# Two layers of a hybrid transformer on one core: row traffic on other queues, modulation weights in half pieces

## The chip, the cores and the metric

The kernel runs on one core of a Trainium2 chip. The metric is the device time of one execution in microseconds (us), taken as the median of the runs. The core has five engines that each work through their own instructions in order and wait for each other by semaphores: TensorE (PE) multiplies matrices into PSUM, VectorE (DVE) and ScalarE (ACT) do element work, GpSimd (POOL) does element work in SBUF, and SyncE (SP) only issues transfers (DMAs). ACT and POOL can issue transfers too. A transfer that has to wait holds up whatever stands behind it on the engine that issues it.

## The reference, cut to what matters

There are 512 latent tokens and 128 context tokens of width 1024, and two layers. In each layer every token gets a modulated normalisation, `rms_norm(x, g) * (1 + scale) + shift`, then one input projection, then four token mixers side by side, then an output projection and a SwiGLU block.

- **Modulation.** `silu(cond) @ w_mod + b_mod` gives six vectors of 1024 per group (shift, scale and gate for both halves of a layer). `w_mod` is 1024 by 6144 per layer, so it is a big weight for two rows of input.
- **Gated DeltaNet.** Keys, queries and values go through a short convolution. Per chunk of 64 tokens a triangular system has to be inverted, and then a scan runs over the chunks. This is a long chain of small steps.
- **Latent attention (MLA).** The input projection gives 256 columns of compressed query, 128 of compressed keys and values and 32 of a rotary key. The first two are RMS-normalised: a row of a token is multiplied by one number for the 256 columns and one for the 128 columns. The 32 columns of the latent tokens are rotated.
- Grouped attention and neighbourhood attention (NA) read further columns of the projection.

All of it is float32.

## The kernel before, in words

Features lie on the partitions and tokens in the free dimension (640 tokens, 512 latent and 128 context). Big products are made as three float32r products of split operands: a weight tile is loaded into `wst`, ACT writes its high part `whi` (line 308) and DVE its low part `wlo` (line 309).

**What sets the order.** The order of TensorE's instructions is written out when the program is built. In the mixer a planner (`_Order`) runs generators as tasks. Each task has a rank (a low one goes first), each step of PE advances a clock, `yield t` lets a task wait for a time of that clock, `yield "w", 1` lets it wait for a PSUM bank, and `od.via(("DMA", 2.8))` books an engine for so long and returns when it is done. PE then works through this order strictly; where an operand is late, PE stands still. The order on the other engines and queues is made by the framework's own scheduler around PE's order. Rank 0 is the DeltaNet chain (`delta_chain`), 0.4 the modulation (`trickle`, layer 0 only), 1.5 the latent rows (`mla_norm`), 2 the rest of the input projection (`rest`).

**Modulation of layer 0** (`modulation`, line 438). A group is 256 columns of `w_mod`, and a piece of it is 512 KB: four blocks of 128 rows, in a tile of 128 x 4 x 256. The product of a piece is four matmuls with a stationary operand of 128 x 32; block i goes to PSUM partitions 32i to 32i+31, so the four of a piece use four different groups of 32 columns of the array. Two pieces add up to a group. Then DVE copies the bank to `msb` (line 481), four small matmuls add the four partial sums, and DVE adds the bias (line 458). Eight groups are done at the start with 16 buffers. The other twelve (24 pieces) are the trickle: it runs beside the mixer of layer 0 with one buffer (`ahead` is 1), so a piece is loaded (line 449, from SP) only when the four matmuls of the piece before are through. The modulation of layer 1 is made by DVE in the SwiGLU block of layer 0.

**Latent rows.** `delta_chain` writes the 416 latent columns of each of five token tiles to DRAM (`craw`, line 813). `mla_norm` (line 1531) later reads them back a tile of 128 tokens at a time into the single buffer `mcr` (line 1541), with 64 columns of rotary table beside them (line 1543). POOL rotates the last 32 columns (lines 1551 to 1553) and scales the other 384 by the two numbers of each row (line 1557). The planner waits 9.0 of its us and takes a bank, PE turns the tile over (`mtp`), ACT scales it into `mst` (lines 1567, 1568), and SP stores it to DRAM (`lat`, lines 1571, 1572, 1574). As `mcr` is single, the load of the next tile waits for these PE transposes. The context tile needs no rotation and stores its rotary key instead (line 1555).

**Other rows.** ACT copies the NA values (`bvst`) and the NA queries and keys (`natst`) out of PSUM, and SP stores them (lines 1921, 1932). SP also loads all weights, so it is one ordered queue for all of this.

Of the kernel before, what the change touches and what calls it, by code (L numbers as in the profile page):

```python
# [287 lines left out]
class _Build:  # L288
# [146 lines left out]
        }  # L435


    def modulation(self, l, groups, ps, pool, ahead, tag="w", lag=False):


        nc, od = self.nc, self.od
        pieces = [(n, j) for g in groups for n in g for j in range(2)]
        there = []

        def load():
            if pieces:
                n, j = pieces.pop(0)
                st = pool.tile([128, 4, 256], F32, tag="wmd", name="wmd", bufs=ahead)
                nc.sync.dma_start(out=st, in_=self.A["wmod"][n, j])
                there.append((st, od.via(("DMA", 2.8)) + 2.2))  # L450

        def finish(g, bank, sb):
            tp = bank[:, 0:4 * len(g)].rearrange("p (e g) -> p e g", g=2)
            for e in range(2 * len(g)):
                self.mm(tp[:, e, :], sb[:, 128 * e:128 * e + 128], self.sel2)
            for q, n in enumerate(g):
                bm = self.par["bmod"][:, l, 2 * n:2 * n + 2]
                nc.vector.tensor_tensor(out=self.mods[l][:, 2 * n:2 * n + 2, :], in0=tp[:, 2 * q:2 * q + 2],
                                        in1=bm.unsqueeze(2).to_broadcast([128, 2, 2]), op=ALU.add)
            od.give(tag, at=od.via(("DVE", 0.1)))  # L460

        for _ in range(ahead):
            load()
        due = None
        for g in groups:
            m = 256 * len(g)
            yield tag, 1
            bank = ps.tile([128, 512], F32, tag=tag, name="mpart")
            for q in range(len(g)):
                for j in range(2):  # L470
                    st, t = there.pop(0)
                    yield t
                    for i in range(4):
                        self.mm(bank[32 * i:32 * i + 32, 256 * q:256 * q + 256], self.sc[:, 4 * j + i, :], st[:, i, :],
                                j == 0, j == 1)
                    load()
                    if due:
                        finish(*due)
                        due = None
            sb = pool.tile([128, m], F32, tag="msb", name="msb", bufs=1)  # L480
            nc.vector.tensor_copy(sb, bank[:, 0:m])
            yield od.via(("DVE", 0.1 + m / 960))
            if lag:
                due = g, bank, sb
            else:
                finish(g, bank, sb)
        if due:
            finish(*due)
# [296 lines left out]
    def delta_chain(self, l, h, S, dn, dt, ps, pd, first):  # L785
# [23 lines left out]
        def sink(t, o):  # L809
            st = self.cv.tile([128, 648], F32, tag="cv", name="crow", bufs=4)  # L810
            nc.scalar.copy(st[:, 0:432], o)
            nc.vector.tensor_copy(g0[:, t], st[:, 416:432])
            nc.sync.dma_start(out=self.dscr["craw"][l, :, t, :], in_=st[:, 0:416])
            for i, (a, b) in enumerate(((0, 256), (256, 384))):
                j = dt.tile([128, 512], F32, tag="mst", name="msq", bufs=1)
                nc.scalar.activation(j[:, 0:b - a], st[:, a:b], AF.Square, accum_out=lss[:, t, i:i + 1])
# [714 lines left out]
    def mla_norm(self, l, dt, ps, S):  # L1531

        nc, A, od = self.nc, self.A, self.od
        yield S["inv"]
        ss = S["lss"]
        nc.vector.tensor_scalar(out=ss[:, :, 1], in0=ss[:, :, 1], scalar1=2.0, scalar2=None, op0=ALU.mult)
        r = dt.tile([128, 5, 2], F32, name="mrs")
        self.rsqrt(dt, r, ss, [128, 5, 2], 1.0 / 256, EPS)
        for t in range(5):
            cr = dt.tile([128, 480], F32, tag="mcr", name="mcr", bufs=1)  # L1540
            nc.sync.dma_start(out=cr[:, 0:416], in_=self.dscr["craw"][l, :, t])
            if t < 4:
                nc.sync.dma_start(out=cr[:, 416:480].rearrange("p (a b) -> p a b", a=2),
                                  in_=A["crope"][:, 512:768].rearrange("p (a t b) -> p a t b", a=2, t=4)[:, :, t])
                x = cr[:, 384:416]
                sw = dt.tile([128, 32], F32, tag="msw", name="msw", bufs=2)
                xv = x.rearrange("p (a b i) -> p a b i", a=2, b=2)
                sv = sw.rearrange("p (a b i) -> p a b i", a=2, b=2)
                sn = cr[:, 448:480].rearrange("p (a b i) -> p a b i", a=2, b=2)
                for b in range(2):  # L1550
                    nc.gpsimd.tensor_tensor(out=sv[:, :, b], in0=xv[:, :, 1 - b], in1=sn[:, :, b], op=ALU.mult)
                nc.gpsimd.tensor_tensor(out=x, in0=x, in1=cr[:, 416:448], op=ALU.mult)
                nc.gpsimd.tensor_tensor(out=x, in0=x, in1=sw, op=ALU.add)
            else:
                nc.sync.dma_start(out=A["okr"][l], in_=cr[:, 384:416])
            for q, (a, b) in enumerate(((0, 256), (256, 384))):
                nc.gpsimd.tensor_scalar(out=cr[:, a:b], in0=cr[:, a:b], scalar1=r[:, t, q:q + 1], scalar2=None, op0=ALU.mult)
            yield od.now + 9.0
            yield "w", 1
            tp = ps.tile([128, 4, 128], F32, tag="w", name="mtp")  # L1560
            for f in range(4):
                w = 128 if f < 3 else 32
                self.turn_over(tp[0:w, f], cr[:, 128 * f:128 * f + w])
            st = dt.tile([128, 512], F32, tag="mst", name="mst", bufs=1)
            sv = st.rearrange("p (f t) -> p f t", f=4)
            for f in range(3):
                nc.scalar.mul(sv[:, f], tp[:, f], self.gcqs[:, l, f:f + 1] if f < 2 else self.par["gckv"][:, l, 0:1])
            nc.scalar.copy(sv[0:32, 3], tp[0:32, 3])
            od.give("w", at=od.via(("ACT", 0.9)))
            lat = self.dscr["lat"][l, :, :, 128 * t:128 * t + 128]  # L1570
            nc.sync.dma_start(out=lat[0:3].rearrange("f p t -> p f t"), in_=sv[:, 0:3])
            nc.sync.dma_start(out=lat[3, 0:32], in_=sv[0:32, 3])
            if t == 4:
                nc.sync.dma_start(out=A["ockv"][l], in_=sv[:, 2])

    def mla_operands(self, l, mp, mk, mt, ats, ps, S):
        nc, A, od = self.nc, self.A, self.od
# [282 lines left out]
    def mixer(self, l, h, h_st, x, fx, fx_st, P, W, p_side, w_side):  # L1860
# [44 lines left out]
        def rest():  # L1905
            for c in range(2):
                yield from self.tm_chunk([A["wtma"][l, c, i] for i in range(2)], h, 256, [(ps, "w")] * 3,
                                         lambda t, o, c=c: nc.scalar.copy(ar[:, t, 256 * c:256 * c + 256], o))
            norms.append(od.spawn(self.gqa_norm(l, ar, dn, dt, S["inv"]), -0.5))
            heads.append(od.spawn(ahead(), 0.3))  # L1910
            for i in range(2):
                o = yield from self.fm_steps(A["wfm"][l, 6 + i], hr, range(KD), ps)
                for hf in range(2):
                    nc.scalar.activation(og[:, i, SPLIT[hf]], o[hf], AF.Silu)
                od.give("w", 2, od.via(("ACT", 0.8)))
            S["gates"].at = od.now + 1.0

            def sink_v(t, o):
                st = self.cv.tile([128, 648], F32, tag="cv", name="bvst", bufs=4)
                nc.scalar.copy(st[:, 0:256], o)  # L1920
                nc.sync.dma_start(out=self.dscr["bv"][l, 128 * t:128 * t + 128], in_=st[:, 0:256])

            yield from self.tm_chunk([A["wtma"][l, 2, i] for i in range(2)], h, 256, [(ps, "w")] * 3, sink_v, "cv")
            for i in range(4):
                o = yield from self.fm_steps(A["wfm"][l, 8 + i], hr, range(KD), ps)
                yield "cv", 1
                od.give("cv", at=od.now + 3.0)
                st = self.cv.tile([128, 648], F32, tag="cv", name="natst", bufs=4)
                for hf in range(2):
                    nc.scalar.copy(st[:, SPLIT[hf]], o[hf])  # L1930
                od.give("w", 2, od.via(("ACT", 0.8)))
                nc.sync.dma_start(out=self.dscr["nat"][l, i], in_=st[:, 0:T])

        def trickle():

            yield S["input"]
            yield from self.modulation(0, [(n,) for n in range(8, 20)], ps, self.cv, 1)
            self.scales(0, 1)

        stacks, pools, norms, heads, last, halves = [], {}, [], [], [], []  # L1940
# [267 lines left out]
```

## Time and profile before

| | |
|---|---|
| median of 3 runs | 1966.07 us (1957.75 to 1971.97) |
| the profiled execution | 1966.56 us, of which the span of its instructions 1964.6 us |
| busy in the span | PE 94%, PE weight load 89%, DVE 55%, ACT 37%, POOL 17% |
| mean granted clock of TensorE | 0.977 of full speed |
| transfers | 213.51 MB, mean 109 GB/s; on the hardware queues 33.3% of 16 engines' time |

The span is made of a start (to about 59 us), the mixer of layer 0 (to about 526), its SwiGLU (to about 960), the mixer of layer 1 (to about 1467) and its SwiGLU. The page of a profile gives the shares of the whole span; the stretches, waits, chain and timelines that the prediction uses are further views of the same execution. A busy PE is not PE at its best, since its instructions are pipelined and the granted clock has two levels (1.2 and 2.4 GHz); "PEclk" is the mean granted clock as a share of the upper one.

### The profile page before, as it was taken

Reading aid. Unit: us, or ns where it says so; the run is one execution under the profiler, and the core shown is the slowest. Engines: PE = TensorE matmul, PEld = TensorE weight load, DVE = VectorE, ACT = ScalarE, POOL = GpSimd, SP = SyncE. Lnnn points to the kernel's source line nnn. Section 1 sums busy time; section 2 is a strip of 40 time slices with the busy share of each in tenths; the row PEclk is TensorE's granted clock in tenths of the full one; section 3 lists DMA queues with packets and bytes.
Section 4 is the critical chain, followed back from the end, with each engine's and each line's share of the span. In section 5 each row is a group of like instructions: output and inputs, shape, how many; then the busy total and the mean of one; then the engine's idle time right before and its main releaser. Section 6 shows DMA issues by size and latency. Waiting matters only on the chain.

```text
span 1964.6 us, 40383 instructions
## 1 busy us (share of the span) xinstructions
PE 1850.0 (94%) x16620; PEld 1745.2 (89%) x16620; DVE 1080.8 (55%) x2312; ACT 734.6 (37%) x1505; POOL 333.3 (17%) x530
## 2 busy tenths in 40 slices
PE   5998998899999999999999999789999999999997
PEld 4986787778899999999988988677889999999997
DVE  6573546677667547657555854667765232233244
ACT  4632124766442112222345323376655221221231
POOL 1221531233310000000133271223321000000001
PEclk9998898999999999999999999899999999999999
DMA  7345422142545435435423422213252222222231
GB/s 298 122 120 136 132 79 93 31 109 79 169 139 172 140 108 193 150 108 190 131 90 100 98 65 66 90 31 95 86 168 78 75 76 75 76 69 82 75 97 54
DMA packets 117624, 213.51 MB, mean 109 GB/s; under 512 B 44544, under 2 KB 65792, under 8 KB 117312
## 3 DMA queue, kind: packets, MB, share of 16 engines
q1 hardware_dynamic: 109376, 205.89, 33.3%
q0 software_dynamic: 2816, 4.72, 1.2%
q8 instruction: 130, 2.13, 0.4%
q10 hardware_dynamic: 5248, 0.33, 0.2%
q14 instruction: 54, 0.44, 0.1%
HBM read 186.29 MB, written 19.89 MB: 105 GB/s over the span
## 4 chain that ended last, share of the span: by engine, by line
PE 79%; DVE 9%; DMA 4%; ACT 4%; issue 2%; SPq 1%; POOL 0%; DVEq 0%; ACTq 0%; POOLq 0%
PE acc L351 57%; PE tacc L351 6%; PE pvo L351 3%; PE ptp L363 3%; PE sc L351 2%; PE invp L351 1%; PE mpart L351 1%; DVE wlo L309 1%; ACT p L1294 1%; DMA wst<-wout 1%; ACT whi L308 1%; DMA wmd<-wmod 1%; PE ysp L351 1%; ACT pt L1329 1%; DVE nq L1770 1%
## 5 line engine op out<-in xcount | busy, mean ns | idle before, releaser
L351 PE MATMUL acc<-h,whi 128*128 128x256 f32 (+1 forms) x3520 | 678.6, 312 | 2.5 <-ACT h L574 1.4
L351 PEld LDWEIGHTS acc<-h,whi 128*128 128x128 f32 x3520 | 578.1, 189 | 11.1 <-issue 3.4
L308 ACT CAST whi<-wst 128x1024 fp32r<-128x1024 f32 (+3 forms) x210 | 203.5, 970 | 699.4 <-PE acc L351 656.8
L351 PE MATMUL acc<-h,wlo 128*128 128x256 f32 (+1 forms) x1760 | 410.5, 310 | 0.8 <-DVE wlo L309 0.8
L309 DVE TENSOR_TENSOR wlo<-wst,whi 128x1024 fp32r<-128x1024 f32 (+3 forms) x210 | 242.0, 1154 | 202.0 <-ACT whi L308 197.1
L351 PEld LDWEIGHTS acc<-h,wlo 128*128 128x128 f32 x1760 | 320.2, 189 | 2.5 <-DVE wlo L309 1.3
L351 PE MATMUL acc<-g,whi 128*128 128x256 f32 (+1 forms) x1128 | 216.5, 309 | 0.0
L541 POOL TENSOR_TENSOR sq<-sq 128x256 f32<-128x256 f32 (+1 forms) x48 | 48.3, 1007 | 926.9 <-ACT sq L535 926.5
L351 PEld LDWEIGHTS acc<-g,whi 128*128 128x128 f32 x1128 | 185.9, 188 | 0.0
L1810 DVE SCALAR_TENSOR_TENSOR x<-acc,mods,x 128x256 f32<-128x256 f32 (+1 forms) x144 | 55.6, 434 | 186.5 <-PE acc L351 186.4
L507 DVE SCALAR_TENSOR_TENSOR wmj<-wmd,cb 128x1024 f32<-128x1024 f32 x112 | 136.9, 1222 | 37.5 <-DMA wmd<-wmodT 36.2
L351 PE MATMUL tacc<-whi,h 128*128 128x256 f32 (+1 forms) x640 | 150.9, 317 | 1.9 <-ACT whi L308 1.5
L351 PE MATMUL acc<-g,wlo 128*128 128x384 f32 (+1 forms) x564 | 135.2, 309 | 0.0
L351 PEld LDWEIGHTS tacc<-whi,h 128*128 128x128 f32 x640 | 111.0, 193 | 12.3 <-issue 6.3
L351 PE MATMUL acc<-oh,whi 128*128 128x384 f32 (+1 forms) x512 | 116.3, 318 | 1.9 <-DVE xe L1810 1.9
L363 PE MATMUL ptp<-cbase,p 128*128 128x128 f32 x512 | 80.7, 284 | 27.0 <-ACT pt L1329 13.0
L351 PEld LDWEIGHTS acc<-g,wlo 128*128 128x128 f32 x564 | 103.3, 188 | 0.0
L351 PE MATMUL tacc<-wlo,h 128*128 128x256 f32 (+1 forms) x320 | 98.2, 307 | 1.3 <-DVE wlo L309 1.3
L363 PEld LDWEIGHTS ptp<-cbase,p 128*128 128x128 f32 x512 | 57.1, 142 | 43.3 <-ACT pt L1329 16.0
L2126 DVE TENSOR_TENSOR sg<-acc,sg 128x256 f32<-128x256 f32 x88 | 39.2, 485 | 101.9 <-PE acc L351 101.9
L1297 POOL TENSOR_SCALAR dg<-cbase,sd 128x128 f32<-128x128 f32 x96 | 58.5, 610 | 206.4 <-DVE sd L1295 147.1
L1294 ACT ACTIVATE p<-sc,sm 128x768 f32<-128x768 f32 (+1 forms) x96 | 79.8, 831 | 31.8 <-DVE sm L1291 23.4
(322 smaller groups left out, 2682.6 us busy)
## 6 DMA issues: line engine op xcount, KB each, us to landing
wmd<-wmodT SPq DMA_DIRECT2D x56, 512.0 KB
wst<-wg SPq DMA_DIRECT2D x44, 512.0 KB
wst<-wu SPq DMA_DIRECT2D x44, 512.0 KB
wmd<-wmod SPq DMA_DIRECT2D x40, 512.0 KB
wst<-wd SPq DMA_DIRECT2D x34, 448.0 KB
wst<-wfm SPq DMA_DIRECT2D x24, 512.0 KB
wst<-wd SPq DMA_DIRECT2D x16, 512.0 KB
wst<-wout SPq DMA_DIRECT2D x28, 256.0 KB
```

Source lines behind the costliest of these rows:

```text
L308: self.nc.scalar.copy(hi, src)
L309: self.nc.vector.tensor_tensor(out=lo, in0=src, in1=hi.bitcast(F32), op=ALU.subtract)
L351: self.nc.tensor.matmul(out, lhsT, rhs, start=start, stop=stop)
L363: self.nc.tensor.transpose(out, in_, self.ident)
L507: nc.vector.scalar_tensor_tensor(out=j, in0=st, scalar=1.0, in1=self.cb[:, g], op0=ALU.mult, op1=ALU.mult, accum_out=self.msum[:, e, g:g + 1])
L541: (eng or nc.gpsimd).tensor_tensor(out=self.sq[hf][0], in0=self.sq[hf][0], in1=sq, op=ALU.add)
L1294: nc.scalar.activation(p, s, AF.Exp, bias=m, accum_out=d)
L1297: nc.gpsimd.tensor_scalar(out=dg, in0=self.ident, scalar1=d, scalar2=None, op0=ALU.mult)
L1329: nc.scalar.copy(pt[:, a:a + m].rearrange("p a b -> p (a b)"), tp[:, :128 * m])
L1770: nc.vector.scalar_tensor_tensor(out=lv, in0=sq[:, bb], scalar=0.125, in1=qv.bitcast(F32), op0=ALU.mult, op1=ALU.subtract)
L1810: self.nc.vector.scalar_tensor_tensor(out=x_out[:, a:b], in0=o[h][:, a - HB * h:b - HB * h], scalar=m[:, 8 * gate + e, grp:grp + 1], in1=x ...
L2126: nc.vector.tensor_tensor(out=sg[:, s], in0=ou[q], in1=sg[:, s], op=ALU.mult)
```

## The change

The change has five parts.

- The load of the latent rows, of the rotary table and the store of the rotary key (lines 1541, 1543, 1555) are issued by POOL instead of SP.
- The stores of the latent columns (813), of the normalised latent (1571, 1572, 1574), of the NA values (1921) and of the NA queries and keys (1932) are issued by ACT instead of SP.
- The scaling of a latent row is a tensor-by-tensor product with the row's number broadcast along the columns, instead of a product with a per-partition scalar.
- The planner's wait after a tile of latent rows is 8.0 of its us instead of 9.0.
- In the trickle a piece is two blocks of 128 rows (256 KB) instead of four, with two buffers instead of one. The SBUF that they take is the same. The planner books 1.4 us of transfer for a half piece instead of 2.8. The modulation at the start keeps its whole pieces and 16 buffers.

```diff
-    def modulation(self, l, groups, ps, pool, ahead, tag="w", lag=False):
+    def modulation(self, l, groups, ps, pool, ahead, tag="w", lag=False, each=4):
-        pieces = [(n, j) for g in groups for n in g for j in range(2)]
+        pieces = [(n, k) for g in groups for n in g for k in range(0, KD, each)]
...
-                n, j = pieces.pop(0)
-                st = pool.tile([128, 4, 256], F32, tag="wmd", name="wmd", bufs=ahead)
-                nc.sync.dma_start(out=st, in_=self.A["wmod"][n, j])
-                there.append((st, od.via(("DMA", 2.8)) + 2.2))
+                n, k = pieces.pop(0)
+                st = pool.tile([128, each, 256], F32, tag="wmd", name="wmd", bufs=ahead)
+                nc.sync.dma_start(out=st, in_=self.A["wmod"][n, k // 4, :, k % 4:k % 4 + each])
+                there.append((st, od.via(("DMA", 0.7 * each)) + 2.2))
...
-                for j in range(2):
+                for k in range(0, KD, each):
                     st, t = there.pop(0)
                     yield t
-                    for i in range(4):
-                        self.mm(bank[32 * i:32 * i + 32, 256 * q:256 * q + 256], self.sc[:, 4 * j + i, :], st[:, i, :],
-                                j == 0, j == 1)
+                    for i in range(each):
+                        r = (k + i) % 4
+                        self.mm(bank[32 * r:32 * r + 32, 256 * q:256 * q + 256], self.sc[:, k + i, :], st[:, i, :],
+                                k < 4, k >= 4)
...
-            nc.sync.dma_start(out=self.dscr["craw"][l, :, t, :], in_=st[:, 0:416])
+            nc.scalar.dma_start(out=self.dscr["craw"][l, :, t, :], in_=st[:, 0:416])
...
-            nc.sync.dma_start(out=cr[:, 0:416], in_=self.dscr["craw"][l, :, t])
+            nc.gpsimd.dma_start(out=cr[:, 0:416], in_=self.dscr["craw"][l, :, t])
             if t < 4:
-                nc.sync.dma_start(out=cr[:, 416:480].rearrange("p (a b) -> p a b", a=2),
+                nc.gpsimd.dma_start(out=cr[:, 416:480].rearrange("p (a b) -> p a b", a=2),
...
-                nc.sync.dma_start(out=A["okr"][l], in_=cr[:, 384:416])
+                nc.gpsimd.dma_start(out=A["okr"][l], in_=cr[:, 384:416])
             for q, (a, b) in enumerate(((0, 256), (256, 384))):
-                nc.gpsimd.tensor_scalar(out=cr[:, a:b], in0=cr[:, a:b], scalar1=r[:, t, q:q + 1], scalar2=None, op0=ALU.mult)
-            yield od.now + 9.0
+                nc.gpsimd.tensor_tensor(out=cr[:, a:b], in0=cr[:, a:b], in1=r[:, t, q:q + 1].to_broadcast([128, b - a]),
+                                        op=ALU.mult)
+            yield od.now + 8.0
...
-            nc.sync.dma_start(out=lat[0:3].rearrange("f p t -> p f t"), in_=sv[:, 0:3])
-            nc.sync.dma_start(out=lat[3, 0:32], in_=sv[0:32, 3])
+            nc.scalar.dma_start(out=lat[0:3].rearrange("f p t -> p f t"), in_=sv[:, 0:3])
+            nc.scalar.dma_start(out=lat[3, 0:32], in_=sv[0:32, 3])
             if t == 4:
-                nc.sync.dma_start(out=A["ockv"][l], in_=sv[:, 2])
+                nc.scalar.dma_start(out=A["ockv"][l], in_=sv[:, 2])
...
-                nc.sync.dma_start(out=self.dscr["bv"][l, 128 * t:128 * t + 128], in_=st[:, 0:256])
+                nc.scalar.dma_start(out=self.dscr["bv"][l, 128 * t:128 * t + 128], in_=st[:, 0:256])
...
-                nc.sync.dma_start(out=self.dscr["nat"][l, i], in_=st[:, 0:T])
+                nc.scalar.dma_start(out=self.dscr["nat"][l, i], in_=st[:, 0:T])
...
-            yield from self.modulation(0, [(n,) for n in range(8, 20)], ps, self.cv, 1)
+            yield from self.modulation(0, [(n,) for n in range(8, 20)], ps, self.cv, 2, each=2)
```

## Rows read from the trace of the kernel before

**Rows 1.** Stretches: their length, busy us (instructions) per engine, clock, DMA share, GB/s.
```profile
59.00:325.00 266.00, 249.05 (x3395) 215.55 (x3395) 143.18 (x394) 83.76 (x193) 72.07 (x132) 0.95 0.38 112
1032.00:1250.00 218.00, 214.00 (x3021) 195.69 (x3023) 130.29 (x335) 80.95 (x187) 77.65 (x130) 0.98 0.28 80
144.00:164.00 20.00, 12.67 (x97) 9.54 (x96) 10.67 (x34) 4.46 (x16) 8.25 (x12) 0.66 0.59 151
225.00:300.00 75.00, 74.33 (x1205) 63.60 (x1205) 35.11 (x116) 19.96 (x51) 22.15 (x46) 1.00 0.30 94
526.00:960.00 434.00, 433.59 (x2949) 432.95 (x2949) 277.94 (x462) 116.85 (x174) 11.48 (x13) 1.00 0.47 148
```

**Rows 2.** Waits of PE from 59 to 325: total us, times, longest.
```profile
PE mtp L363 <- POOL mcr L1557: 6.2, 1, 6.2
PE mpart L351 <- DMA wmd<-wmod: 4.8, 3, 2.4
...
PE tacc L351 <- DVE wlo L309: 0.6, 1, 0.6
```

**Rows 3.** Timeline of SP, of POOL and of DVE around the wait for the latent rows.
```profile
144.09 0.33 SPq L1541 DMA_DIRECT2D mcr<-dcraw  x1
...
146.72 5.01 POOL L1557 TENSOR_SCALAR mcr<-mcr,mrs 128x256 f32<-128x256 f32 x2 [10.40 <-DMA mcr<-dcraw]
151.70 0.40 POOL L1551 TENSOR_TENSOR msw<-mcr 128x16 f32<-128x16 f32 x2
...
150.32 0.43 DVE L1049 TENSOR_TENSOR ivw<-ivv,ivx 104x30 f32<-104x30 f32 x1
154.28 0.42 DVE L481 COPY msb<-mpart 128x256 f32<-128x256 f32 x1 [3.53 <-PE mpart L351]
```

**Rows 4.** Chain that ended last: start, us, what.
```profile
99.05 0.86 PE decp L351 x2
...
123.36 0.57 PE mpart L351 x8
...
153.20 1.06 PE mpart L351 x8
...
164.91 3.79 DMA wmd<-wmod
```

**Rows 5.** Groups of instructions: those on `wmd` from 59 to 330.
```profile
L449 SPq DMA_DIRECT2D wmd<-wmod x23: 327/328/1016, 88.1 to 250.3; - x23
```

**Rows 6.** Groups on POOL by shape: busy us, mean ns, idle before them.
```profile
L1557 POOL TENSOR_SCALAR mcr<-mcr,mrs 128x256 f32<-128x256 f32 x10 | 17.0, 1696 | 63.2 <-DMA mcr<-dcraw 56.4 <-DVE mrs L383 3.5 <-DVE gc L911 3.2
...
L1193 POOL TENSOR_TENSOR kd<-kt,ksc 128x128 f32<-128x128 f32 x40 | 16.0, 425 | 54.0 <-PE spp L351 54.0
...
L1197 POOL TENSOR_TENSOR st<-st,egl 128x256 f32<-128x256 f32 x18 | 12.3, 683 | 15.2 <-DVE rsa L381 6.0 <-DVE ors L383 5.2 <-ACT st L1229 3.1
...
L1652 POOL DMA_DIRECT2D mq<-mqr x16 | 8.1, 511 | 5.8 <-ACT mqr L308 5.0 <-PE sc L351 0.8
...
L1557 POOL TENSOR_SCALAR mcr<-mcr,mrs 128x128 f32<-128x128 f32 x10 | 7.0, 701 | 0.0
```

**Rows 7.** Timeline of POOL at the same place of layer 1.
```profile
1116.42 5.75 POOL L1557 TENSOR_SCALAR mcr<-mcr,mrs 128x256 f32<-128x256 f32 x2 [9.84 <-DMA mcr<-dcraw]
1122.14 1.33 POOL L1551 TENSOR_TENSOR msw<-mcr 128x16 f32<-128x16 f32 x2
```

**Rows 8.** Transfers by issue: engine, count, KB each, us to landing.
```profile
mk<-mkrs POOLq DMA_DIRECT2D x16, 96.0 KB, 2.2
...
mq<-mqr POOLq DMA_DIRECT2D x16, 64.0 KB, 3.8
```

**Rows 9.** Transfers that ACT issues before: shortest, median, longest ns of an issue.
```profile
L1025 ACTq DMA_DIRECT2D dinv<-dM x8: 310/542/708, 112.4 to 1088.9; - x8
```

**Rows 10.** Stretches of 25 us in which DVE is full, columns as in Rows 1.
```profile
125.00:150.00 25.00, 19.97 (x147) 19.44 (x145) 24.86 (x80) 9.60 (x24) 3.69 (x7) 0.99 0.39 125
...
1100.00:1125.00 25.00, 24.72 (x191) 24.43 (x190) 24.62 (x77) 11.48 (x29) 8.59 (x9) 1.00 0.31 93
```

## The prediction

> **What bounds the kernel now.** I first read the stretches [rows 1]. The two SwiGLU blocks, 897 us of the span, keep PE busy without a gap at the full clock (434 us of it is shown), and nothing of the change lies there. The mixers are left, up to the point where attention starts, and there the two layers can be held against each other: layer 0 with the trickle takes 266 us, layer 1 without it 218. PE stands idle 266.00 - 249.05 = 16.95 us in the first and 4.0 in the second. Its clock gives away another (1 - 0.95) x 266 = 13.3 us and (1 - 0.98) x 218 = 4.4. So layer 0 loses some 30 us and layer 1 some 8, 22 of the 48 us between them; the rest is work, the trickle's own above all. What can be won by filling gaps is therefore in layer 0, and about 20 us (30.3 less layer 1's 8.4 stretched by 266/218).
>
> Then the waits of PE in that stretch [rows 2]: the largest is one of 6.2 us for a latent row (`mtp` for the scaling on POOL), the second 4.8 us in three pieces for modulation weights. The timeline shows the first from the other side [rows 3]: SP issues the load at 144.09, right after the transposes of the tile before; POOL gets the row at 146.72 and takes 5.01 us for two products. DVE is drawn in: its inverse stops at 150.75 and waits 3.53 us for a `msb` that stands behind the transposes on PE. From 144 to 164 the granted clock is 0.66 of full, so PE ran most of that stretch at the lower of its two levels, 1.2 GHz, after standing idle; the same eight trickle matmuls took 1.06 us at 153.20 and 0.57 at 123.36 [rows 1, 4].
>
> **The change part by part.** The sum is made against the profiled execution, 1966.56 us (span 1964.6 and 1.96 around it), 0.5 above the median shown, so I use the same result for both.
>
> 1. *Trickle waits.* With one buffer a piece is asked for when the last is used up, and lands 3.79 us later in the chain [rows 4]. With two, one half is on its way while the other is used. I take the 4.8 us as gone; the ends are 0 (PE just meets the next half too early) and -4.8. SP issues 24 more loads (24 pieces become 48; 23 of the 24 fall into rows 5) at 0.33 us, 8 us of a queue that loses more than that in 6.
>
> 2. *The latent row that PE waits for.* Before, from the load's issue to the scaled row: 144.09 to 151.73, 7.64 us. After, three terms on POOL. The issue: 0.51 us, from POOL's present issues [rows 6]. The landing: 2.2 to 3.8 us, medians of POOL's own transfers [rows 8]; I take the middle, 3.0. The scaling: tensor-by-tensor products of 256 and 128 columns take 0.683 and 0.425 us, 1.1 together [rows 6], while scaling takes 1.70 + 0.70 on average, pulled up by two slow pairs (5.01 and 5.75) where DVE is full [rows 3, 7, 10]. Tensor products suffer there too: a pair of 16 columns took 1.33 us against 0.40 [rows 3, 7]. So 1.1 + 0.9 = 2.0, with ends 1.1 and 1.1 + 3.4 = 4.5 (the slowest pair, 5.75, less the average of 2.4). Sum 0.5 + 3.0 + 2.0 = 5.5, a gain of 2.1; ends 3.8 and 8.8, from -3.8 to +1.2. The planner's 8.0 for 9.0 only lets PE arrive up to 1 us earlier at the same wait: zero. In layer 1 PE doesn't wait here, so nothing is won.
>
> 3. *The clock.* 144 to 164 gives away 0.34 x 20 = 6.8 us [rows 1]. A shorter wait may keep the clock up or not; nearest is the wait itself, of which a third goes: -2, ends 0 and -6.8.
>
> 4. *What halving costs on PE.* This is the part that speaks against the change. A whole piece uses four groups of 32 columns, two passes each (x8 in the row), and takes 0.57 us. One pass of 512 columns takes 0.43 (0.86 for two [rows 4]), so one of 256 takes 0.215, and the eight would take 1.72 one after the other: the four groups run beside each other. A half piece has two groups, each still with two passes that must follow each other, 0.43 us, plus some start. I take 0.50, between 0.43 and the 0.57 of a whole piece. 48 x 0.50 - 24 x 0.57 = +10.3 us of PE work. Ends: 0, if two halves come back to back and share the array, and +13.7, if each costs a whole. Half of it I put into gaps that stay (some 17 - 7 us idle, most of it where the trickle runs): +5.
>
> 5. *Issues on ACT.* 50 stores move to it (per layer 5 of `craw`, 10 of `lat` and 1 of the normalised latent, 5 of `bv`, 4 of `nat`), each 0.31 to 0.54 us of ACT's own order [rows 9]: 16 to 27 us. ACT is busy 83.8 of 266 and 81 of 218 us; that idle time hides them. Queued behind each store are the PSUM copies of the scan, and PE waits for these. During the scan (225 to 300) PE is idle only 0.67 us and ACT 55 of 75, so I take +1. If every one of the 14 stores per layer that fall there (5 of `bv`, 4 of `nat`, 5 of the last two latent tiles) delayed the chain it would be 28 x 0.54 = +15; below nothing there is no reason to go.
>
> 6. *SP's queue.* 70 issues leave it, with their waits for ACT and PE, and 24 come. What stands behind them are weight loads, and PE waited only 0.6 us for split weights [rows 2]: zero, end -0.6. Earlier loads then meet the modulation pieces, at a DMA share of 0.38.
>
> 7. *POOL.* 20 issues x 0.51 = +10 us, scaling 10 x (2.4 - 1.1) = -13 us, on an engine busy 72 of 266: zero. The load for the next tile now holds POOL's order until PE has turned the last one; behind it stand only instructions of the same row or ones that already stood behind its scaling.
>
> Sum: -4.8 - 2.1 - 2 + 5 + 1 = -2.9, so **1963.7 us**, say 1963.
>
> **A rule of the skill against the change.** DVE is busy 24.86 of the 25 us around the critical load, and 24.62 in layer 1 [rows 10]; POOL's products were slow just there [rows 3, 7]. The Trainium skill, SBUF — State Buffer (SBUF: two separate sides), says that a DMA issued by GpSimd has its descriptors written by GpSimd, which is locked out while VectorE runs in a mode that uses both ports, and advises the SP or ACT queue instead. By that rule term 2 would be a loss; no POOL transfer of the kernel before lies under so full a DVE, so no row decides. It is the third rival.
>
> **The rivals.**
>
> *The trickle leaves early and the gaps close* (faster). By the planner's own numbers a whole piece takes 0.6 + 2.8 + 2.2 = 5.6 us from one to the next, two halves with two buffers 0.6 + 1.4 + 2.2 = 4.2. 24 pieces then end 24 x 1.4 = 34 us earlier; the last is now loaded at 250 [rows 5]. If layer 0 then fills PE as layer 1 does, the 20 us above go, plus a little from 2: 1944. For it: layer 1 reaches that fill. Against: term 4, and that part of the 17 us lies in a place where DVE's inverse is what is waited for. Chance 0.22.
>
> *Halves run alone on the array* (slower). Place: PE between 87 and 260 us. Price: +13.7, if each half costs 0.57 and none of it falls into a gap, because the waits of 1 and 2 were only moved. 1966.6 + 13.7 = 1980. It decides once a half takes over (13.7 + 7)/48 = 0.43 us outside gaps: then the 6.9 us of terms 1 and 2 are paid back. Against: halves whose weights are there may run together. Chance 0.18.
>
> *POOL can't issue under a full DVE* (as the rule says). The load asked for at 144.1 goes out when DVE stops at 150.75, lands 3.0 later and is scaled in 1.1: 154.9 instead of 151.7, +3.2 in place of -2.1, and term 3 falls away: 1963.7 + 5.3 + 2 = 1971. Chance 0.12.
>
> *It does nothing.* As the order of all queues is made anew, the waits come back under other names and the sum is zero, 1966. Chance 0.10.
>
> The forecast has 0.38.
>
> **How the numbers follow.** 1% of this time, 19.7 us, is about what a measurement can tell from no change: below 1946 and above 1986. The forecast's own range is 1955 to 1972 (terms 1 to 3 lost or doubled, 4 at either end). To 1944 it takes in half of the first rival, to 1982 the second at its price and the start of term 5's end: 1944 to 1982 leaves out about 0.11 below and 0.08 above. Faster by over 1%: two thirds of the first rival and a tail of the forecast, 0.2. Slower: a third of the second, and term 5 near its end, 0.12. The rest, 0.68, within 1%.
>
> **What would show it.** Step 1: PE's waits for `wmd` are gone. Step 2: the latent row's load goes out on POOL and the scaling takes about 2 us at the same place; PE's wait for `mtp` is near 4 us. Step 3: the stretch around it has a clock above 0.66. Step 4: in the chain a half piece takes near 0.50 us with four instructions; 0.3 or less would refute it, and pieces that end far before 250 with a fuller PE would speak for the first rival. Step 5: new waits of PE for ACT in the scan. Step 6: none for weights. A difference that lies in SwiGLU or in attention would mean that the prediction looked in the wrong place.

## The result and the profile after

The kernel after takes 1978.12 us (median of 12 runs, 1974.5 to 1985.4), the kernel before beside it 1965.22 (12 runs): ratio 1.0069, 95% interval [1.0055, 1.0082]. It is 0.7% slower, some 13 us, where 1963 was forecast. The profiled execution of after has a span of 1973.6 us, 9.0 more than before.

I cut each profile at four events that every kernel has: the first `tacc` product of a layer (its mixer begins) and its first `sc` product (attention begins). The two mixers before, and then mixer 0, the stretch between, mixer 1 and the stretch that [rows 1] showed at 0.66 of the clock, after (length, busy us per engine, clock):

```profile
58.00:323.50 265.50, 248.59 (x3393) 215.11 (x3393) 142.68 (x392) 83.26 (x193) 72.07 (x132) 0.95 0.38 112
...
1031.20:1266.20 235.00, 220.34 (x3152) 200.92 (x3152) 141.28 (x368) 84.66 (x195) 78.52 (x132) 0.96 0.28 81
```

```profile
58.10:330.10 272.00, 255.69 (x3393) 213.70 (x3393) 144.61 (x392) 84.30 (x194) 73.15 (x141) 0.96 0.37 109
330.10:1036.30 706.20, 679.06 (x4951) 656.14 (x4949) 453.50 (x858) 280.17 (x553) 91.89 (x132) 0.99 0.42 130
1036.30:1279.10 242.80, 223.62 (x3153) 203.52 (x3153) 141.87 (x368) 84.83 (x195) 78.77 (x141) 0.95 0.27 79
144.00:164.00 20.00, 7.87 (x63) 7.37 (x61) 12.67 (x33) 5.21 (x13) 0.17 (x3) 0.71 0.55 112
```

Layer 0's mixer grew by 6.5 us and layer 1's by 7.8; the two stretches behind them shrank by 1.5 (707.7 before) and 3.9 (698.4 to 694.5): together the 9.0 of the spans. In layer 0 it is work, not waiting: PE is busy 7.1 us longer and stands idle 16.3 us, before 16.9.

Most of that work is the modulation. The tile view of the weight pieces from 59 us on (shortest, median, longest ns of an instruction; first and last start), one half piece of the chain, and the group on PE:

```profile
L351 PE MATMUL mpart<-wmd,sc x192: 377/403/636, 86.1 to 234.4; 128*32 128x256 f32 x192
L450 SPq DMA_DIRECT2D wmd<-wmod x46: 327/328/1228, 86.8 to 229.4; - x46
...
116.12 0.56 PE mpart L351 x4
...
L351 PE MATMUL mpart<-wmd,sc 128*32 128x256 f32 x192 | 28.3, 411 | 1.7 <-DMA wmd<-wmod 1.7
```

A half piece takes 0.56 us with its four instructions, a whole one 0.57 with eight [rows 4]. The same 192 instructions keep PE busy 28.3 us; before it was 16.66. The other work of the mixer took some 4.5 us less (11.6 against the 7.1 in all). The loads end at 229 us instead of 250 [rows 5].

The waits of PE in layer 0's mixer (59 to 331) and, behind the line of dots, in layer 1's (1036 to 1279): total, times, longest.

```profile
PE invp L351 <- DVE ivr L1089: 12.3, 1, 12.3
PE mpart L351 <- DMA wmd<-wmod: 1.7, 4, 0.7
...
PE otp L351 <- DVE dno L1271: 8.0, 1, 8.0
PE mtp L363 <- POOL mcr L1559: 3.0, 1, 3.0
PE mtp L363 <- POOL mcr L1555: 2.5, 1, 2.5
```

Against [rows 2] the wait for the latent row (6.2) is gone and the weights went from 4.8 to 1.7, but one wait of 12.3 us has come where PE stood before. In layer 1 two waits for a latent row are new (the 8.0 for `dno` was 8.9 before).

The place of the 12.3, on PE and then on SP and DVE:

```profile
151.23 0.64 PE L351 MATMUL mpart<-wmd,sc 128*32 128x256 f32 x8
164.15 1.93 PE L351 MATMUL invp<-ivr,dM 32*32 32x32 f32 x128 [12.29 <-DVE ivr L1089]
166.01 1.08 PE L351 MATMUL mpart<-wmd,sc 128*32 128x256 f32 x8
...
152.98 0.69 SPq L1060 DMA_DIRECT2D dinv<-ivw  x2
155.74 5.04 SPq L1063 DMA_DIRECT2D rt<-dinv  x8
...
151.92 1.03 DVE L1057 COPY ivw<-ivv 40x1024 f32<-40x1024 f32 x1
163.65 1.43 DVE L1089 STREAM_TRANSPOSE ivr<-rt 128x256 f32<-128x256 f32 x4 [6.54 <-DMA rt<-dinv]
```

DVE's inverse ends at 152.95, goes out to memory and back as `rt`, and is turned into `ivr` at 163.65. PE's order has the product on it next, and everything ready stands behind it. In the kernel before PE turned a latent tile at this place (with its wait of 6.2) and multiplied pieces, convolution sums and gram blocks; its first product on `ivr` came at 177.1, long after `ivr` was there (167.54). In after the latent rows no longer stand here: the first of them, turned at 143.5 before, is turned at 246.1.

### The profile page after: what moved, and what is told of

It is laid out like the page before. It is cut to its first block, busy times and chain, and to the rows that moved or that the text cites. A ratio compares the mean times of both kernels' runs of the same rounds, so it can differ in the third digit from the quotient of the medians.

```text
span 1973.6 us, 40410 instructions
## 1 busy us (share of the span) xinstructions
PE 1856.9 (94%) x16620; PEld 1743.4 (88%) x16620; DVE 1083.8 (55%) x2312; ACT 734.9 (37%) x1505; POOL 336.2 (17%) x550
## 4 chain that ended last, share of the span: by engine, by line
PE 78%; DVE 9%; DMA 5%; ACT 4%; issue 2%; POOL 1%; SPq 1%; DVEq 0%; ACTq 0%; POOLq 0%
PE acc L351 56%; PE tacc L351 6%; PE pvo L351 2%; PE ptp L363 2%; PE sc L351 2%; PE mpart L351 2%; DVE wlo L309 1%; PE invp L351 1%; DMA wst<-wout 1%; DVE sm L1293 1%; ACT p L1296 1%; ACT whi L308 1%; DMA wmd<-wmod 1%; PE spp L351 1%; PE ysp L351 1%
```

## The experiments

Ratios are to the kernel before, run beside each on the same chip, with their 95% interval; its own median was between 1965.2 and 1969.3 us, so the ratios are compared and not the medians. Where one ratio is taken from another, "uncertain by" is the root of the summed squares of half their intervals.

**e1: whole pieces again.** The kernel after with

```diff
-                pieces = [(n, k) for ... for k in range(0, KD, each)]
+                pieces = [(n, j) for ... for j in range(2)]
...
-            yield from self.modulation(0, ..., self.cv, 2, each=2)
+            yield from self.modulation(0, ..., self.cv, 1)
```

> The changed kernel with whole modulation pieces and one buffer, as before; the queues, the product and the 8.0 stay. Array theory (a half piece takes as long on PE as a whole one, 0.56 us against 0.57, so 48 halves cost 13 us more than 24 wholes): some 6 us faster than the changed kernel, that is the part of the loss that lies before layer 1, near 1972; PE's wait for wmd comes back. POOL-queue theory (the load of a latent row stands in POOL's order, and layer 1's wait for mtp of 5.5 us comes from it): layer 1 keeps its wait for mtp, 5 us over before, 1970 to 1972. If the halves did no harm: no faster than the changed kernel, 1978.

1970.06 us, ratio 0.9999 [0.9986, 1.0012]. Mixer 0 takes 260.9 us and the pieces 16.2 us of PE; mixer 1 stays at 243.9, with 5.1 us of waits for `mtp`. What is left of the change is neutral: 4.6 us won in layer 0, 8.9 lost in layer 1's mixer, most of the difference given back behind the mixers (the span is 1.5 us longer than before).

**e2: half pieces alone**, on the kernel before:

```diff
-            yield from self.modulation(0, ..., self.cv, 1)
+            yield from self.modulation(0, ..., self.cv, 2, each=2)
```

> The kernel before with only the half pieces and two buffers. Array theory: slower than before by 5 to 8 us, 1971 to 1973, all of it before layer 1; a half piece near 0.56 us in the chain; PE's waits for wmd under 2 us. POOL-queue theory alone: no slower than before, 1965, or faster by the 4.8 us of wmd waits, 1960.

1974.77 us, ratio 1.0026 [1.0012, 1.0040]. Mixer 0 takes 272.8, the pieces 28.4 us of PE, idle 16.4; there is no wait for `mtp` in layer 1. The halves cost some 5 us by themselves, net of the trickle waits that they take away (1.6 us left of 4.8). They also make layer 0's new order by themselves: here too the first latent row is turned late, at 247.8, and PE waits 12.5 us for `ivr`, with all row traffic as before.

**e3: halves cut along the columns**, four groups of 32 columns kept, on the kernel after (the weights lie in memory cut in the same way):

```diff
-                st = pool.tile([128, each, 256], ...)       # two slices of k, 256 columns
+                st = pool.tile([128, 4, wide], ...)         # four slices of k, wide = 128 columns
...
-                        self.mm(bank[32 * r:32 * r + 32, 256 * q:256 * q + 256], ...)
+                        self.mm(bank[32 * i:32 * i + 32, 256 * q + wide * c:256 * q + wide * c + wide], ...)
```

> The changed kernel with the same bytes per half piece and the same two buffers, but halved along the columns: four blocks of 128 rows by 128 columns, so that all four groups of array columns work, each for half the columns. PE's order of instructions is that of the changed kernel. Array theory: a half piece takes about 0.30 us in place of 0.56, 48 x 0.26 = 12 us less PE work, and the time falls by 6 to 12 us, 1966 to 1972. If the loss came from the number of pieces, their transfers or the order of PE: no change, 1978.

1977.54 us, ratio 1.0038 [1.0020, 1.0057]. The pieces take 20.3 us of PE instead of 28.3 and mixer 0 268.1; the wait for `ivr` is 9.0 and the one for weights 5.0. The ratio is 0.31% below that of after (uncertain by 0.23), some 6 us, though the two medians are alike: the kernel before took 1967.7 us beside this run. That speaks for array time of the halves that lies at least in part on the path; the 1966 to 1972 expected were not reached.

**e4: latent loads back on SP**, and the load of the rotary table and the store of `okr` with them (one of three lines, on the kernel after):

```diff
-            nc.gpsimd.dma_start(out=cr[:, 0:416], in_=self.dscr["craw"][l, :, t])
+            nc.sync.dma_start(out=cr[:, 0:416], in_=self.dscr["craw"][l, :, t])
```

> The changed kernel with the loads of the latent rows, of the rotary table and the store of the rotary key issued by SP again; PE's order is that of the changed kernel. POOL-queue theory: layer 1's wait of PE for mtp (5.5 us) falls to about 0.6, the time by about 5, 1973. Array theory alone: no change, 1978. If what matters is that PE comes to mtp earlier by the planner's 8.0: the wait stays, 1978.

1977.79 us, ratio 1.0054 [1.0033, 1.0074]. Layer 1's wait for `mtp` is still 4.5 us: GpSimd's queue doesn't make it; with the 8.0 kept the wait stays.

**e5 and e6: the planner's number.** e5 is e1 with 9.0; e6 is the kernel before with 8.0 and nothing else:

```diff
-            yield od.now + 9.0
+            yield od.now + 8.0
```

> The kernel after with whole pieces and one buffer again, and with the planner's 9.0 for the latent scaling; queues and product stay as after. PE's order is then that of the kernel before. Theory (the 8.0 makes the order in which layer 1 waits for a latent row): PE's wait for mtp in layer 1 goes from 5.1 us (whole pieces with 8.0) to 0, and the time falls by about 5, to 1962-1966, ratio 0.997 to 0.999 to the kernel before; layer 0 keeps the one wait for a latent row, shortened from 6.2 to about 4. Rival (the product or POOL's queue makes that wait): 4 to 5 us of mtp stay in layer 1, and the time stays at 1970.

> The kernel before with the planner's 8.0 for 9.0, nothing else. Theory (8.0 makes the order that waits): PE waits 3 to 6 us for mtp in layer 1, where the kernel before has none, and the time is 1968 to 1972. Rival (product or queue): no wait for mtp in layer 1, time 1963 to 1968.

e5: 1965.12 us, ratio 1.0003 [0.9987, 1.0020], no wait for `mtp` in layer 1, mixer 1 235.6. Against e1 (0.9999) the time didn't fall by the 5 us expected. e6: 1976.33 us, ratio 1.0059 [1.0038, 1.0080], mixer 1 241.8 with this wait (PE, start, us):

```profile
1175.03 0.49 PE L363 MATMUL mtp<-cbase,mcr 128*128 128x128 f32 x3
1179.69 0.39 PE L363 MATMUL mtp<-cbase,mcr 128*32 128x128 f32 x1 [4.17 <-POOL mcr L1553]
```

One number of the planner, with the same instructions on the same queues, makes the kernel slower by 0.6%, more than the 1968 to 1972 expected. PE's order differs in layer 1 alone: the transposes of the fourth latent row stand ahead of products of `tacc` and of the inverse which they followed before. In the kernel after the same place reads:

```profile
1174.47 0.28 PE L351 MATMUL tacc<-whi,h 128*128 128x256 f32 x1
1177.70 0.69 PE L363 MATMUL mtp<-cbase,mcr 128*128 128x128 f32 x3 [2.95 <-POOL mcr L1559]
1180.85 0.40 PE L363 MATMUL mtp<-cbase,mcr 128*32 128x128 f32 x1 [2.46 <-POOL mcr L1555]
1181.18 1.19 PE L351 MATMUL invp<-ivr,dM 32*32 32x32 f32 x29
```

In the kernel before that tile was turned at 1181.50, without a wait, right among `tacc` products. The wait costs clock as well. In the 26 us from this place on (columns as above; before, e6, after) PE stands idle 0.2, 4.2 and 5.4 us, and behind the wait it runs at the lower level for longer: the last two `tacc` products that together take 0.63 us, and not 0.40, come 9, 21 and 22 us behind the place.

```profile
1170.70:1196.70 26.00, 25.81 (x429) 23.69 (x428) 8.13 (x23) 8.57 (x24) 8.87 (x14) 0.87 0.25 81
...
1175.10:1201.10 26.00, 21.83 (x286) 20.58 (x286) 4.69 (x12) 6.26 (x19) 5.96 (x9) 0.67 0.18 54
...
1174.60:1200.60 26.00, 20.59 (x262) 19.22 (x261) 4.75 (x12) 5.60 (x17) 8.09 (x16) 0.67 0.15 46
```

The trace of e6 doesn't put the whole loss there, though: of the 10.0 us that its span is longer, mixer 1 has 6.8, and mixer 0, in the order of before, 7.9 (273.4 us at a clock of 0.93); the other stretches are shorter.

**e7 and e8: halves on all four groups.** The loads, buffers and bytes of after; on the array two slices of k by two column halves fill four groups. e7 has 8.0, e8 9.0. The partial sums lie elsewhere in the bank and are added accordingly (not shown). PE's order is not quite that of after, since the planner books these products otherwise.

```diff
                     for i in range(each):
-                        r = (k + i) % 4
-                        self.mm(bank[32*r:32*r+32, 256*q:256*q+256], self.sc[:, k+i, :], st[:, i, :], k < 4, k >= 4)
+                        for c in range(2):      # the numbers put in for each = 2
+                            r = 2 * c + i
+                            self.mm(bank[32*r:32*r+32, 128*q:128*q+128], self.sc[:, k+i, :],
+                                    st[:, i, 128*c:128*c+128], k == 0, k == KD - 2)
```

> The kernel after, but each half piece (two of the eight slices of k, contiguous as after) is cut along its columns on the array alone: two slices by two column halves fill all four groups of 32 columns, so a half takes four products of 128 columns at once instead of two of 256. Loads, buffers, queues, product and the 8.0 stay. Theory (a half costs a whole piece because two groups stand empty, and all of it lies on the path): a half takes 0.27 to 0.35 us, busy time of the products of wmd in layer 0 falls from 28.3 to 15-20 us, and the time by 7 to 12, to 1967-1971. Rival (the order and the pacing cost the time, the array's cost would be idle time otherwise): busy time falls as much, PE's idle time in layer 0 grows from 16.3 by about that, and the time stays within 3 us of 1978.

> The same with the planner's 9.0. Theory (8.0 makes layer 1's wait): the 5.5 us wait for mtp in layer 1 goes and the time is another 5 lower, 1962 to 1966, below the kernel before. Rival (product or POOL's queue): the wait stays and the time is that of the kernel with 8.0.

e7: 1977.14 us, ratio 1.0058 [1.0038, 1.0078]; e8: 1968.64, ratio 1.0019 [1.0005, 1.0034]. In e7 a half that stands alone takes 0.36 us in the chain (0.56 in after), all of them 21.2 us of PE, mixer 0 264.2. Its tile view, beside that of after above:

```profile
L352 PE MATMUL mpart<-wmd,sc x384: 269/297/423, 85.7 to 228.3; 128*32 128x128 f32 x192
```

So 7 us of array time were won back in the trace, and the time didn't follow (1967 to 1971 expected; the ratio is 0.11% below that of after, uncertain by 0.24). In the trace mixer 0 is 7.8 us shorter, though PE now waits 11.2 us for weights, since the wait for `ivr` is gone; the stretch behind it is 5.6 us longer (711.8 against 706.2), and why was not found. With 9.0 another 8 us go, as expected in kind; the 1962 to 1966 expected were not reached. That e8's profile has 1958.9 us of span, 8 below what its median asks for, says how much one execution may differ.

**e9: the kernel after with 9.0**, nothing else. PE's order is then that of e2.

```diff
-            yield od.now + 8.0
+            yield od.now + 9.0
```

> The kernel after with the planner's 9.0, nothing else; PE's order is then that of the kernel before with half pieces alone. Theory (two costs: the halves some 5 us, the 8.0 the rest): the wait for mtp in layer 1 goes from 5.5 us to 0, layer 1 up to attention falls from 242.8 to 234-238 us, layer 0 stays at 270-273, the time is 1967 to 1972, ratio 1.001 to 1.003. Rival (the halves alone make the kernel after slower, its 8.0 costs nothing in sum): the time stays at 1977-1978, ratio near 1.007.

1970.60 us, ratio 1.0011 [0.9997, 1.0026]. Mixer 1 has no wait for `mtp` and takes 236.2, mixer 0 268.3 with the wait for `ivr` at 11.6:

```profile
55.00:323.30 268.30, 252.31 (x3379) 209.82 (x3379) 145.68 (x392) 84.78 (x194) 72.64 (x141) 0.97 0.38 111
1035.50:1271.70 236.20, 221.90 (x3153) 202.45 (x3153) 141.29 (x368) 84.68 (x195) 77.14 (x141) 0.96 0.29 81
```

Undoing one number gives back 0.58% of the 0.69% (uncertain by 0.20). Against e8, which has the same 9.0 and 7.7 us less array time (20.9 against 28.6), it is no slower (1.0011 against 1.0019), but the two orders differ.

**e10: whole pieces with 13.0**, the queues and the product as after; **e11: e8 with 10.0.**

```diff
-            yield od.now + 8.0
+            yield od.now + 13.0      # e11: 10.0
```

> The kernel after with whole pieces, one buffer and the planner's number at 13.0: PE's transposes of a latent row are put later behind its scaling. Theory (a number nearer to what the row takes takes PE's wait for it away): no wait for mtp in layer 0 (5.5 us with 9.0) nor in layer 1, layer 0 up to attention 256-260 us, time 1958 to 1963, ratio 0.996 to 0.999, faster than both kernels. Rival (the order is only made anew, other waits come): some other wait of 3 to 6 us in layer 0 and the time at 1965 or above.

> The kernel after with its halves on all four groups of the array and the planner's 10.0. Theory (as with 9.0, with the row's wait still less likely): no wait for mtp in either layer, time 1964 to 1969. Rival (the order made anew decides): one of the layers is 5 us or more longer than with 9.0 (264.4 and 229.9), time 1970 or above.

e10: 1962.94 us, ratio 0.9966 [0.9945, 0.9986]: faster than both kernels, by 0.3% than the kernel before. Its mixers (rows as above) and PE's waits in layer 0:

```profile
56.10:314.20 258.10, 245.65 (x3395) 213.48 (x3394) 143.00 (x392) 83.61 (x193) 73.88 (x141) 0.96 0.40 115
1025.90:1259.00 233.10, 218.94 (x3153) 199.61 (x3153) 140.76 (x368) 84.56 (x195) 76.23 (x141) 0.97 0.29 82
...
PE mpart L351 <- DMA wmd<-wmod: 6.2, 6, 3.9
PE mpart L351 <- DVE msb L481: 2.5, 2, 1.5
```

No wait for a latent row is left in either layer's mixer. e11: 1968.36 us, ratio 1.0000 [0.9983, 1.0018], no wait for `mtp`; with 10.0 mixer 1 is 237.5 and with 9.0 229.9, in one trace each and at clocks of 0.95 and 0.98; the time isn't longer.

**e12: the row stores alone on ScalarE's queue** (50 issues, one of six lines shown, on the kernel before):

```diff
-            nc.sync.dma_start(out=self.dscr["craw"][l, :, t, :], in_=st[:, 0:416])
+            nc.scalar.dma_start(out=self.dscr["craw"][l, :, t, :], in_=st[:, 0:416])
```

> The kernel before with the row stores alone on ScalarE's queue (50 issues); PE's order is that of before. Theory (ACT's idle time hides them): ratio 0.999 to 1.001, PE's waits for ACT in the mixers grow by less than 2 us. Rival (PE's copies wait behind the issues): PE's waits for ACT grow by 5 us or more, ratio 1.003 or above.

1965.63 us, ratio 0.9978 [0.9961, 0.9995]. PE's waits for ACT in the mixers don't grow: none in layer 0 in either kernel, 1.0 us in layer 1 (1.5 + 0.3 before). Term 5's upper end is out; there is a small gain if anything. Its mixer 0 has PE's order of before and took 272.6 us at a clock of 0.92, against 265.5 at 0.95: a mixer's length in one profile can be off by 7 us through the clock alone, and only the waits are firmer (the pieces' busy time is 18.3 us there against 16.7).

**e13 to e15: which layer pays for 8.0.** e13 has 8.0 in layer 1 only, e14 in layer 0 only, both on after; e15 is whole pieces with 8.0 in layer 1 only.

```diff
-            yield od.now + 8.0
+            yield od.now + (9.0, 8.0)[l]      # e13, e15;  (8.0, 9.0)[l] in e14
```

> The kernel after with the planner's 8.0 in layer 1 only, 9.0 in layer 0. Theory (the 8.0 costs its 11 us in layer 1, where PE's transposes of the fourth latent row are put ahead of products that were ready): a wait of 4 to 6 us for mtp in layer 1, layer 1 up to attention 240 to 244 us, time 1974 to 1979, ratio 1.004 to 1.007. Rival (layer 0 pays, where 8.0 makes another order of half pieces): time 1968 to 1972, ratio near 1.001 as with 9.0 in both.

> The kernel after with 8.0 in layer 0 only, 9.0 in layer 1. Theory (layer 1 pays): no wait for mtp in layer 1, ratio near 1.001, time 1968 to 1972. Rival (layer 0 pays): layer 0 272 us or more, ratio 1.004 to 1.007, time 1974 to 1979.

> The kernel after with whole pieces and one buffer, 8.0 in layer 1 only; PE's order is that of whole pieces with 8.0 in both. Theory (layer 1's order costs the same with whole pieces): ratio 1.004 to 1.007 where whole pieces with 9.0 had 1.0003, time 1974 to 1978. Rival (the wait in layer 1 is given back behind it, and 8.0 only costs where pieces are halves): ratio 0.998 to 1.002, as whole pieces with 8.0 had (0.9999), though PE waits 5 us for mtp in layer 1.

e13: 1978.60 us, ratio 1.0043 [1.0022, 1.0064], waits for `mtp` of 4.6 us in layer 1, mixer 1 242.3. e14: 1972.70, 1.0025 [1.0006, 1.0045], no such wait, mixer 1 232.1. e15: 1967.46, 0.9994 [0.9972, 1.0015], though PE waits 4.5 us in layer 1 (mixer 240.3). With halves, 8.0 costs 0.32% in layer 1 (e13 less e9, uncertain by 0.26) and 0.14% in layer 0 (e14 less e9, uncertain by 0.24). The first is clear of noise, but the two are not clear of each other; the wait and the longer mixer 1 go with the 8.0 of layer 1. With whole pieces and the new row traffic the wait is there and the time is not.

## Why the prediction was wrong

The runs walk from before to after in three steps: halves +0.26% (e2), then GpSimd loads, ACT stores and product together -0.15% (e9 less e2, 1.0011 - 1.0026, uncertain by 0.20), then 8.0 for 9.0 +0.58% (after less e9, uncertain by 0.20). On 1966 us that is +5, -3 and +11.

**The step that failed most is the end of step 2**: "The planner's 8.0 for 9.0 only lets PE arrive up to 1 us earlier at the same wait: zero. In layer 1 PE doesn't wait here, so nothing is won." I priced the number as a shift in time and left out that a planner turns it into an order. It put the fourth latent row of layer 1 ahead of products that were ready, PE runs in order, and PE now waits 3.0 + 2.5 us where it had waited 0. The fourth rival speaks of an order made anew but prices it at zero. By itself the number costs 0.59% (e6), within the kernel after 0.58% (e9), 11 of the 13 us. Of the 7.8 us by which mixer 1 grew 4.5 are idle time and 3.3 are busy time, in the main the lower clock behind the wait; where the rest of the 11 arises was not found.

**Step 4 was mis-sized**: +10.3 us of PE's work for what the trace shows as +11.7 (28.3 - 16.7), and half of that put into gaps. The half piece took 0.56 us, not 0.50: two groups take as long as four. And the gaps took none of it: idle time is 16.3 us after and 16.9 before. Halves alone cost 5 us (e2) net of 3.2 us of weight waits that they take away, so the term was nearer 8 than 5 (an estimate from these two). This is the second rival's mechanism at its price on the array (13.7 worked out, 48 x 0.56 - 24 x 0.57 = 13.2 by the chain). That its 1980 lies near the 1978 measured is luck: with the same halves and 9.0 the kernel takes 1970.60 (e9).

**Step 1** was right in kind: 4.8 became 1.7 (expected 0). **Step 2's** wait for the row went away in layer 0, but not by a faster row: the halves moved the rows 100 us later (e2). Where the order of before is kept, the step's sum held: in e5 POOL issues the load at 143.06 and has scaled the row at 148.51, 5.45 us where I had 5.5, and PE's longest wait for it is 4.0 (near 4 forecast).

```profile
143.06 0.58 POOL L1541 DMA_DIRECT2D mcr<-dcraw  x1 [8.05 <-PE mtp L363]
146.48 2.07 POOL L1557 TENSOR_TENSOR mcr<-mcr,mrs 128x256 f32<-128x256 f32 x2 [2.14 <-DMA mcr<-dcraw]
```

In the kernel after the same terms are in this timeline of POOL in layer 1, as in [rows 7]:

```profile
1117.65 0.58 POOL L1543 DMA_DIRECT2D mcr<-dcraw  x1 [7.25 <-PE mtp L363]
1118.23 0.72 POOL L1545 DMA_DIRECT2D mcr<-crope  x1
1120.42 4.90 POOL L1559 TENSOR_TENSOR mcr<-mcr,mrs 128x256 f32<-128x256 f32 x2 [1.47 <-DMA mcr<-dcraw]
...
1138.58 0.96 POOL L1559 TENSOR_TENSOR mcr<-mcr,mrs 128x256 f32<-128x256 f32 x2 [1.58 <-DMA mcr<-dcraw]
```

From the load's issue to the first product it takes 2.77 us, and I had 0.5 + 3.0. A pair of products takes 0.96 us (scaling by a column took 1.50 us for the tile after that of [rows 7], 1134.52 in the kernel before) but 4.90 where DVE runs the inverse, above my upper end of 4.5 and not the 2.0 taken. **Step 3**: the stretch went from 0.66 to 0.71, of little worth, since PE stands idle in it for 12.3 us. That wait is the fourth rival's sentence, "the waits come back under other names": it holds for layer 0's idle time.

**Step 5**: the upper end is out, and the term has the wrong sign if any (e12, which also takes these stores off SP: -0.22%, between -0.39 and -0.05, where I had +1 us and nothing below zero). **Step 6** held: `tacc` still waits 0.6 us for `wlo`. **Step 7** held, and the third rival fell: POOL issued at 1117.65, right behind the transposes of 1116.76, with DVE busy 23.06 of the 25 us around it:

```profile
1110.00:1135.00 25.00, 25.00 (x271) 24.68 (x270) 23.06 (x67) 10.65 (x27) 7.23 (x11) 1.00 0.43 104
```

In layer 0, at the rival's own place, e5's load was used 3.42 us after its issue, with DVE busy 24.90 of the 25 us from 124 on. The rule of the Trainium skill, SBUF — State Buffer (SBUF: two separate sides), that GpSimd can't write the descriptors of its DMAs while VectorE runs in a mode that uses both ports, shows no delay here; no row tells whether VectorE ran in such a mode. With the loads back on SP (e4) the kernel is no faster that can be measured. It is POOL's products, not its issues, that were slow there (4.90 us against 0.96). DVE was full around both pairs (5.00 of the 5.00 us from 1120.40, 1.10 of the 1.10 from 1138.50), in the main with two-input products of the inverse and the convolution around the slow one, with transposes and reductions around the fast one. The same section of the Trainium skill says that a GpSimd instruction and a VectorE instruction with two SBUF inputs hold a shared pair of ports against each other for a whole instruction; the trace agrees with that in kind, but no run here took the products of DVE away.

**The first rival** (leave early, close the gaps) had its condition and not its effect: the pieces end 23 us earlier (234 against 257), and the idle time is what it was. Filler was not missing when the inverse made its round trip: 120 of the 192 piece products still lay behind the first product on `ivr` in PE's order, and `tacc` products with them. The order put that product first. That halves alone make such an order is shown (e2); which booking of the planner does it was not tested.

**What stays open.** The costs don't add up in every pairing. With whole pieces, product and GpSimd loads, 8.0 costs nothing that can be measured (e1 0.9999 and e15 0.9994 against e5 1.0003), though PE waits 4.5 to 5.1 us for `mtp` in layer 1; e1 has the very order of PE that costs 0.59% in e6, where the row traffic is that of before. Some of the wait comes back behind the mixer (the stretch from attention to the end is 695.4 and 695.1 us, 698.7 in e5), but in e6 it does too (696.0 against 698.4). So 8.0 makes the order, and the wait with it, in every pairing; why the time follows in some and not in others was not found. Nor is it known which of e10's parts bring its 0.3%, or how much of the 5 us of halves is array time and how much order.

## What to carry to other kernels

A number in a planner is a change of the order: build the order with the old and the new number and read which instruction of an in-order engine moves ahead of which, before pricing the number as time. A wait can go because the order changed and come back under another name, so compare an engine's total idle time, not the wait by name. Cutting a piece of matmuls in two along the dimension that fills the array's column groups halved the use of the array, not the time: cut it so that all groups stay filled, or leave it whole. Here whole pieces did best: neither way of filling the groups (e3, e8) was faster than the kernel before.

## What was unexpected of the hardware

- Two groups of 32 columns with 256 columns of float32 take 0.56 us in the chain, four groups 0.57; four groups with 128 columns take 0.36 (e7), when they stand alone. The time fell with the columns that each group streams and not with the number of groups.
- A pair of tensor products on POOL took 0.96 us and 4.90 us, 18 us apart, with DVE full both times; the slow one lies where DVE runs the two-input products of the inverse.
- A transfer issued by POOL beside a full DVE was used 2.77 us after its issue; its issue and that of the rotary table behind it took 0.58 and 0.72 us of POOL.
- Over 26 us that begin with the waits of PE for a latent row in layer 1 (5.4 us idle) the granted clock was 0.67; at the same place without them it was 0.87.
